# Three early up weights are split later at the norm of the output projection, in a two-layer hybrid decoder trunk

## The chip, the cores and the metric

The kernel runs on one core of one Trainium2 chip. The metric is the device time of one execution in microseconds (us). Five engines work side by side, each through its own queue in order: TensorE (PE: matrix products and transposes; its weight loads are listed as PEld), VectorE (DVE), ScalarE (ACT), GpSimd (POOL) and SyncE (SP), whose queue issues the loads from the chip's main memory here. An instruction that has to wait holds up everything behind it on its engine.

## The reference

The reference computes two layers on 512 tokens of width 1024, in float32. In each layer the residual stream goes through one input projection into three mixers (latent attention, causal pooling, a matrix-memory recurrence), whose outputs meet in one output projection. Then come a layer norm and a gated MLP, and a second norm:

```
mix = concat([a, p, m]) @ w_out[l]
h = layer_norm(ALPHA * h + mix, ln1_g[l], ln1_b[l])
a, g = split(h @ w_up[l], 2)            # 1024 -> 2 * 2816
g = causal_dwconv(g, w_fconv[l], b_fconv[l])
h = layer_norm(ALPHA * h + (silu(g) * a) @ w_down[l], ln2_g[l], ln2_b[l])
```

The change concerns the place between the second and the third of these lines: the norm behind the output projection, and the first products of the up projection.

## The kernel before

**Numbers in two parts.** A float32 product is made of three products: each operand is split into a high part (a cast on ScalarE to a shorter format) and a low part (VectorE subtracts the high part from the original), and high x high, high x low and low x high are added up. Activations are split by `split` (lines 187 to 189) into `a_hi` and `a_lo`, weights by `fetch` (lines 149 to 170).

**Weights.** All weights stand in one list in the order of their use. `getw` (line 174) hands out the next one and calls `fetch` for all up to `ahead` beyond it. `fetch` makes three instructions on three engines: a 512 KB load on SyncE's queue into a buffer `raw` (two buffers), the cast to `hi` on ScalarE (line 168), the subtraction to `lo` on VectorE (line 169). There are four `hi` and four `lo` buffers. A load waits for the `raw` buffer, which the subtraction of the weight two places earlier frees.

**The norm.** The 512 tokens are four tiles of 128, counted from 0. The second half of the output projection ends tile by tile, and for each tile `ln_tail` (line 208) follows: mean and variance on VectorE, the power -1/2 on GpSimd (line 200), the normalisation on VectorE (line 227), and then, twice (once for each half of the 1024 columns): four transposes on TensorE into one bank (line 238), four activations on ScalarE into a buffer `lnt` that apply gain and bias (line 243; two such buffers), and the split into `a_hi` (ScalarE, line 188) and `a_lo` (VectorE, line 189).

**The first up weights.** The up projection starts before all four tiles are normalised. `t_half` (line 313) takes the first four weights of the list, here called A, B, C and D. In its first half (`hf` 0) each is multiplied with tiles 0 and 1, in the second half (`hf` 1) with tiles 2 and 3. Each weight and half has two groups of four blocks (the first needs the first halves of the two tiles, the second their second halves), and each group three passes of four products: `hi` with `a_hi`, `lo` with `a_hi`, `hi` with `a_lo` (line 328). A is fetched earlier, during the output projection (`ahead=1` there). B, C and D are fetched in `t_half` itself, each just ahead of its first products, inside a `tc.issue_after` block.

**What sets the order.** The order of TensorE's instructions is that in which the program traces them; a small planner (`Order`) interleaves the generators by estimated costs. On the other engines the framework's scheduler sets the order when the program is built: of the instructions that are ready by its own clock it takes the one traced first, unless `high_priority` moves one forward (the norm's statistics and normalisation have that). `tc.issue_after(ins)` adds an edge of order, without a wait, to `ins` from each instruction that the block traces on the engine of `ins`, and leaves those on other engines alone. In `t_half` it names `last_rs[0]`, the last power that `rstd_of` gave to GpSimd.

Of the kernel before, what the change touches and what calls it, by code (L numbers as in the profile page):

```python
# [10 lines left out]
F32 = mybir.dt.float32  # L11
# [3 lines left out]
ALU = mybir.AluOpType  # L15
# [3 lines left out]
P = 128  # L19
# [82 lines left out]
def trunk(ctx: ExitStack, tc: tile.TileContext, I: dict, out: bass.AP, layers=DEPTH):  # L102
    nc = tc.nc
    V, A, G, T = nc.vector, nc.scalar, nc.gpsimd, nc.tensor
# [11 lines left out]
    a_hi = pers.tile([P, NT, KD, P], F32R, name="a_hi")  # L116
    a_lo = pers.tile([P, NT, KD, P], F32R, name="a_lo")
# [18 lines left out]
    def mmc(n):  # L136
        return n / 2400.0 + 0.003

    def bank(name):
        return psum.tile([P, S], F32, tag="ps", name=name)  # L140
# [33 lines left out]
    def getw(name, ahead=1):  # L174
        while len(wloaded) <= min(used[0] + ahead, len(wlist) - 1):
            fetch()
        hi, lo, nm = wloaded[used[0]]
        assert nm == name, (nm, name)
        used[0] += 1
        return hi, lo  # L180
# [4 lines left out]
        T.matmul(o, wlo, xhi, start=False, stop=stop)  # L185

    def split(hi, lo, src, eng=None):
        A.copy(hi, src)
        (eng or V).tensor_tensor(lo, src, hi.bitcast(F32), ALU.subtract)

    def load_gb(pool, gsrc, bsrc, name):
        gb = pool.tile([P, 2, D], F32, tag="gb", name="gb_" + name)
# [4 lines left out]
    def rstd_of(dst, src, eps):  # L197
        n = src.shape[1]
        V.tensor_scalar_add(dst, src, eps)
        return G.tensor_tensor(dst, dst, nhalf[:, :n], ALU.pow).ins  # L200
# [3 lines left out]

    dve_free = [0.0]
    last_rs = [None]

    def ln_tail(pool, h, i, st, gb, cols, name, transpose=True, dst=None, pre=1.3):
        mv = small.tile([P, 2], F32, tag="mv", bufs=4, name="mv_" + name)
        rs = small.tile([P, 1], F32, tag="rs", bufs=4, name="rs_" + name)  # L210
        with tc.high_priority(offset=2000):
            V.bn_aggr(mv, st)
            last_rs[0] = rstd_of(rs, mv[:, 1:2], LN_EPS)
        z = h[:, i, :]
        if not transpose:
            n = D // 2 if i == NT - 1 else D
            with tc.high_priority(offset=1000 if i == NT - 1 else 0):
                for a in range(0, D, n):
                    za = z[:, a : a + n]
                    V.scalar_tensor_tensor(za, za, mv[:, 0:1], gb[:, 0, a : a + n], ALU.subtract, ALU.mult)  # L220
                for a in range(0, D, n):
                    za = z[:, a : a + n]
                    V.scalar_tensor_tensor(za, za, rs[:, 0:1], gb[:, 1, a : a + n], ALU.mult, ALU.add)  # L223
                    (A if a else nc.sync).dma_start(dst[i * P : (i + 1) * P, a : a + n], za)
            return
        with tc.high_priority(offset=2000):
            V.tensor_scalar(z, z, mv[:, 0:1], rs[:, 0:1], ALU.subtract, ALU.mult)
        if dst is not None:
            nc.sync.dma_start(dst[i * P : (i + 1) * P, :], z)
        dve_free[0] = max(dve_free[0], sch.now) + pre + 1.5  # L230
        yield 0.0, dve_free[0] + 0.72 - sch.now, None
        for q in range(2):
            tp = bank("tp_" + name)
            t = pool.tile([P, S], F32, tag="lnt", bufs=2, name="lnt_" + name)
            for k in range(4):
                f = q * 4 + k
                ks = slice(k * P, (k + 1) * P)
                T.transpose(tp[:, ks], h[:, i, f * P : (f + 1) * P], ident)
            for k in range(4):
                f = q * 4 + k  # L240
                ks = slice(k * P, (k + 1) * P)
                w, b = cols[:, f : f + 1], cols[:, KD + f : KD + f + 1]
                A.activation(t[:, ks], tp[:, ks], AF.Identity, bias=b, scale=w)
            split(a_hi[:, i, q * 4 : q * 4 + 4, :], a_lo[:, i, q * 4 : q * 4 + 4, :],
                  t.rearrange("p (k t) -> p k t", t=P))
            yield 0.43, 0.0, None
        sch.set(f"hT_{name}_{i}", 3.82)

# [64 lines left out]
    def t_half(names, waits):  # L313
        ws, os_ = [], []
        for hf in range(2):
            t0, t1 = hf * 2, hf * 2 + 2
            for w in waits[hf]:
                yield 0.0, 0.0, w
            for n, nm in enumerate(names):
                if hf == 0:  # L320
                    with tc.issue_after(last_rs[0]):
                        ws.append(getw(nm, ahead=0))
                    os_.append(bank("t_" + nm))
                hi, lo = ws[n]
                for k0 in range(0, KD, 4):
                    for p_ in range(3):
                        for k in range(k0, k0 + 4):
                            T.matmul(os_[n][:, t0 * P : t1 * P], (lo if p_ == 1 else hi)[:, k * P : (k + 1) * P],  # L328
                                     (a_lo if p_ == 2 else a_hi)[:, t0:t1, k, :], start=k == p_ == 0,
                                     stop=k == KD - 1 and p_ == 2)  # L330
                    yield 12 * mmc(256), 0.0, None
                if hf == 1:
                    yield ("done", n, os_[n])
# [97 lines left out]
    for i in range(NT):  # L431
        for a in range(0, D, D // 2 if i == 0 else D):
            n = D // 2 if i == 0 else D
# [14 lines left out]
    def first_norm():  # L448
        for i in range(NT):
            st = new_stats("0")  # L450
            for j in range(2):
                ln_stats(h, i, j, st)
            yield from ln_tail(lp, h, i, st, None, cols0, "in0", dst=spill)
            if i == 0:
                warm(6)
# [28 lines left out]
    for l in range(layers):  # L484
# [31 lines left out]
        def rms(i, ps, n, gcol, hi, lo, nm):  # L516
            kd = None
            if nm == "cq":
                o = QL + 2 * MH
                kd = t2("kd")[:, : 2 * P]  # L520
                m1, m2 = kd[:, 0:ROPE], kd[:, ROPE : 2 * ROPE]
                V.tensor_mul(m1, ps[:, o : o + ROPE], cst_t[:, i, 0, :])
                V.tensor_mul(m2[:, 0:32], ps[:, o + 32 : o + 64], cst_t[:, i, 1, 0:32])
                V.tensor_mul(m2[:, 32:64], ps[:, o : o + 32], cst_t[:, i, 1, 32:64])
                V.tensor_tensor(kd[:, P : 2 * P].rearrange("p (a e) -> p a e", a=2),
                                m1.unsqueeze(1).to_broadcast([P, 2, ROPE]),
                                m2.unsqueeze(1).to_broadcast([P, 2, ROPE]), ALU.add)
            sq = t2("sq_" + nm)
            ss = small.tile([P, 1], F32, tag="ss", bufs=4, name="ss_" + nm)
            A.activation(sq[:, :n], ps[:, :n], AF.Square, scale=n ** -0.5, accum_out=ss)  # L530
            rs = small.tile([P, 1], F32, tag="rsq", bufs=4, name="rs_" + nm)
            rstd_of(rs, ss, RMS_EPS)
            V.scalar_tensor_tensor(sq[:, :n], ps[:, :n], rs[:, 0:1], gqkv[:, gcol : gcol + n], ALU.mult, ALU.mult)
            yield 0.0, 4.0 + 0.7 * i, None
            tp = bank("rt_" + nm)
            for k in range(n // P):
                T.transpose(tp[:, k * P : (k + 1) * P], sq[:, k * P : (k + 1) * P], ident)
            if kd is not None:
                T.transpose(tp[:, QL : QL + P], kd[:, P : 2 * P], ident)
                ts_ = slice(i * P, (i + 1) * P)  # L540
                split(kp_hi[:, ts_], kp_lo[:, ts_], tp[:, QL : QL + P])
            split(hi[:, :, i * P : (i + 1) * P], lo[:, :, i * P : (i + 1) * P],
                  tp[:, :n].rearrange("p (k t) -> p k t", t=P))
            yield n / P * 0.107, 0.0, None
            sch.set(f"{nm}{l}_{i}", 2.94)
# [498 lines left out]
        def ffn_main():  # L1044
            yield from until(o0)
            for y in out_gen(1):
# [4 lines left out]
                if last_grp and y[0] > 0 and pre_left:  # L1051
                    with tc.issue_after(lo_ins[f"o{l}_1_3"]):
                        hbox["pre"](pre_left.pop(0), 1)
            ffn_open()
            hbox["g1"] = load_gb(hp, I["ln1_g"][l], I["ln1_b"][l], "1")
            w1 = [[f"hT_a{l}_{i}" for i in range(2 * hf, 2 * hf + 2)] for hf in range(2)]
            yield from consume(t_half([f"up{l}_0_0", f"up{l}_0_1", f"up{l}_1_0", f"up{l}_1_1"], w1),
                               lambda n, o: up_consume(n // 2, n % 2, o))
            for n in range(4, 2 * NF):
# [116 lines left out]
```

## Time and profile before

| | us |
|---|---|
| three timed runs | 1143.2, 1141.77, 1143.14; median 1143.14 |
| the profiled execution | 1142.44 |
| its span, first to last instruction | 1140.7 |
| TensorE busy | 1118.5 (98%) |
| VectorE busy | 783.4 (69%) |
| ScalarE busy | 506.1 (44%) |
| GpSimd busy | 276.6 (24%) |

The stage of the change lies around 205 to 250 us in layer 0 and around 764 to 806 us in layer 1.

How to read it: the page's first part gives busy time, share of the span and number of instructions of each engine. A timeline lists instructions in order of time: start, duration, engine, line, operation, tile written and tiles read, and how many like ones were merged (x4); brackets hold the idle time of the engine ahead of the row, and what ended it. Matmuls overlap, so the pace is read from the starts, not from the durations. The chain of waits follows the work that ended last back through what released it. A table of windows gives, for stretches of time, the busy time of each engine and the granted clock of TensorE (1.00 is 2.4 GHz, 0.50 is 1.2 GHz). `t_up` are the banks of the up products, `hi_up`, `lo_up` and `raw_up` the up weights, `tp_a` the transposes of this norm.

### The profile page before, as it was taken

To read this page: it belongs to the slowest core of one execution; us is meant where nothing else is said; L and a number is where in the kernel's file an instruction comes from. 1 tells how busy PE (TensorE), PEld (TensorE's weight loads), DVE (VectorE), ACT (ScalarE), POOL (GpSimd) and SP (SyncE) were. 2 spreads that over 40 slices of the span, in tenths; PEclk is the share of its full clock that TensorE was granted. 3 is DMA by queue.
4 is the path that set the end of the run, shared out by engine and by line. 5 is a ranking of instruction groups with operands and counts; after the bars stand their busy time and mean duration, and the time that the engine had idled before them with its cause. 6 is when DMAs were issued, how large, how long until landed. Compare 5 with 4: busy or idle time off the path is not lost. (4 is left out here: it accounts for less than half of the span.)

```text
span 1140.7 us, 14294 instructions
## 1 busy us (share of the span) xinstructions
PE 1118.5 (98%) x5399; PEld 930.2 (82%) x5399; DVE 783.4 (69%) x1151; ACT 506.1 (44%) x870; POOL 276.6 (24%) x218
## 2 busy tenths in 40 slices
PE   8999999999999999999999999999999999999996
PEld 5878778798888888888887888888888888888885
DVE  6776886856696667844568669685777865696447
ACT  6664552553443444333266645517434334443320
POOL 1316500128320222011003362000663012220111
PEclk9999999999999999999999999999999999999999
DMA  8332215323415231433243213062432343215221
GB/s 302 107 107 63 88 38 203 126 78 93 140 60 191 90 109 58 129 125 97 92 155 130 66 34 110 24 243 67 120 122 91 118 154 98 93 56 166 93 74 74
DMA packets 36084, 124.96 MB, mean 110 GB/s; under 512 B 4521, under 2 KB 5033, under 8 KB 36017
## 3 DMA queue, kind: packets, MB, share of 16 engines
q1 hardware_dynamic: 35872, 123.80, 33.0%
q8 instruction: 42, 0.69, 0.3%
q10 hardware_dynamic: 144, 0.26, 0.1%
q14 instruction: 26, 0.21, 0.1%
HBM read 117.74 MB, written 6.31 MB: 109 GB/s over the span
## 5 line engine op out<-in xcount | busy, mean ns | idle before, releaser
L183 PE MATMUL t_up<-a_hi,hi_up 128*128 128x512 f32 x640 | 249.0, 389 | 0.0
L184 PE MATMUL t_up<-a_lo,hi_up 128*128 128x512 f32 x640 | 249.0, 389 | 0.0
L185 PE MATMUL t_up<-a_hi,lo_up 128*128 128x512 f32 x640 | 249.0, 389 | 0.0
L169 DVE TENSOR_TENSOR lo_up<-raw_up,hi_up 128x1024 fp32r<-128x1024 f32 x88 | 129.2, 1469 | 103.5 <-ACT hi_up L168 102.4
L168 ACT CAST hi_up<-raw_up 128x1024 fp32r<-128x1024 f32 x88 | 92.4, 1050 | 120.5 <-PE t_up L184 70.4
L184 PEld LDWEIGHTS t_up<-a_lo,hi_up 128*128 128x128 f32 x640 | 120.1, 188 | 25.0
L183 PEld LDWEIGHTS t_up<-a_hi,hi_up 128*128 128x128 f32 x640 | 120.1, 188 | 24.8
L185 PEld LDWEIGHTS t_up<-a_hi,lo_up 128*128 128x128 f32 x640 | 120.1, 188 | 24.8
L995 POOL TENSOR_TENSOR s_lo<-y,s_hi 128x256 fp32r<-128x256 f32 (+1 forms) x32 | 48.5, 1516 | 282.3 <-ACT s_hi L994 261.9
L972 ACT ACTIVATE y<-y 128x512 f32<-128x512 f32 x44 | 27.8, 632 | 107.4 <-DVE y L971 107.4
L971 DVE SCALAR_TENSOR_TENSOR y<-t_up,pp,y 128x511 f32<-128x511 f32 x88 | 65.5, 744 | 11.5 <-ACT y L969 10.2
L976 DVE TENSOR_TENSOR y<-y,t_up 128x512 f32<-128x512 f32 x44 | 30.2, 687 | 52.9 <-PE t_up L185 37.4
L980 POOL TENSOR_TENSOR f_lo<-y,f_hi 128x512 fp32r<-128x512 f32 x12 | 21.1, 1755 | 176.3 <-ACT f_hi L979 176.3
L169 DVE TENSOR_TENSOR lo_s<-sum,hi_s 128x1024 fp32r<-128x1024 f32 x32 | 43.3, 1354 | 14.6 <-ACT hi_s L168 14.6
L293 PE MATMUL o<-hi_o,a_hi 128*128 128x512 f32 x128 | 50.9, 398 | 0.0
L295 PE MATMUL o<-hi_o,a_lo 128*128 128x512 f32 x128 | 49.9, 390 | 0.0
L294 PE MATMUL o<-lo_o,a_hi 128*128 128x512 f32 x128 | 49.9, 390 | 0.0
L1033 PE MATMUL dx<-hi_s,s_hi 128*128 128x512 f32 x128 | 49.8, 389 | 0.0
L1034 PE MATMUL dx<-lo_s,s_hi 128*128 128x512 f32 x128 | 49.8, 389 | 0.0
L1035 PE MATMUL dx<-hi_s,s_lo 128*128 128x512 f32 x128 | 49.8, 389 | 0.0
L168 ACT CAST hi_s<-sum 128x1024 fp32r<-128x1024 f32 x32 | 33.6, 1052 | 30.3 <-PE dy L1035 13.4
L168 ACT CAST hi_s<-raw_s 128x1024 fp32r<-128x1024 f32 x24 | 25.3, 1055 | 39.9 <-PE dx L1035 21.5
(311 smaller groups left out, 2545.6 us busy)
## 6 DMA issues: line engine op xcount, KB each, us to landing
raw_up<-in_w_up_dram SPq DMA_DIRECT2D x88, 512.0 KB, 3.5
raw_s<-in_w_ds_dram SPq DMA_DIRECT2D x32, 512.0 KB, 3.5
raw_o<-in_w_out_dram SPq DMA_DIRECT2D x16, 512.0 KB, 3.5
raw_it<-in_w_it_dram SPq DMA_DIRECT2D x12, 512.0 KB, 3.6
raw_d<-in_w_dn_dram SPq DMA_DIRECT2D x12, 512.0 KB, 3.4
spill<-h SPq DMA_DIRECT2D x8, 512.0 KB, 4.0
raw_ib<-in_w_ib_dram SPq DMA_DIRECT2D x8, 512.0 KB, 3.5
h<-spill SPq DMA_DIRECT2D x8, 512.0 KB, 7.8
```

Of the source, the lines that this page charges most:

```text
L168: A.copy(h_, r_)
L169: lo_ins[name] = eng.tensor_tensor(l_, r_, h_.bitcast(F32), ALU.subtract).ins
L183: T.matmul(o, whi, xhi, start=start, stop=False)
L184: T.matmul(o, whi, xlo, start=False, stop=False)
L185: T.matmul(o, wlo, xhi, start=False, stop=stop)
L293: T.matmul(o, xhi, whi, start=at == 0, stop=False)
L294: T.matmul(o, xhi, wlo, start=False, stop=False)
L295: T.matmul(o, xlo, whi, start=False, stop=at == nk - 1)
L971: V.scalar_tensor_tensor(y[:, t:], o[:, : S - t], w(2 - t), y[:, t:], ALU.mult, ALU.add)
L1033: T.matmul(o, xhi, hi[:, w], start=new and pp == 0, stop=False, skip_group_check=True)
L1034: T.matmul(o, xhi, lo[:, w], start=False, stop=False, skip_group_check=True)
L1035: T.matmul(o, xlo, hi[:, w], start=False, stop=end, skip_group_check=True)
```

## The change

`split` returns its two instructions, and `ln_tail` keeps those of the last half of each tile in `tile_split`. In `t_half` the block around the fetch of the first weight (A, which is there already) keeps the edge to `last_rs[0]`. For the second to fourth weight (B, C, D) the edges go to the two instructions of tile 1's last split: their casts on ScalarE are queued behind that tile's last cast, and their subtractions on VectorE behind its last low part. The loads on SyncE's queue get no edge.

```diff
     def split(hi, lo, src, eng=None):
-        A.copy(hi, src)
-        (eng or V).tensor_tensor(lo, src, hi.bitcast(F32), ALU.subtract)
+        a = A.copy(hi, src).ins
+        return a, (eng or V).tensor_tensor(lo, src, hi.bitcast(F32), ALU.subtract).ins
...
     last_rs = [None]
+    tile_split = {}
...
-            split(a_hi[:, i, q * 4 : q * 4 + 4, :], a_lo[:, i, q * 4 : q * 4 + 4, :],
-                  t.rearrange("p (k t) -> p k t", t=P))
+            tile_split[i] = split(a_hi[:, i, q * 4 : q * 4 + 4, :], a_lo[:, i, q * 4 : q * 4 + 4, :],
+                                  t.rearrange("p (k t) -> p k t", t=P))
...
             for n, nm in enumerate(names):
                 if hf == 0:
-                    with tc.issue_after(last_rs[0]):
+                    with ExitStack() as hs:
+                        for ins in tile_split[1] if n else (last_rs[0],):
+                            hs.enter_context(tc.issue_after(ins))
                         ws.append(getw(nm, ahead=0))
```

## Rows read from the trace of the kernel before

**Rows 1.** The page, part 1: busy us, share of the span, instructions.

```profile
PE 1118.5 (98%) x5399; PEld 930.2 (82%) x5399; DVE 783.4 (69%) x1151; ACT 506.1 (44%) x870; POOL 276.6 (24%) x218
```

**Rows 2.** The chain of waits, layer 1's norm: start, us, what.

```profile
782.31 0.61 DVE a_lo L189
782.96 3.60 PE t_up L328 x28
```

**Rows 3.** Timeline of TensorE, layer 0: passes 1, 4, 6, 10, transposes, passes 14, 48.

```profile
219.07 0.72 PE L328 MATMUL t_up<-a_hi,hi_up 128*128 128x256 f32 x4
...
221.55 0.74 PE L328 MATMUL t_up<-a_hi,hi_up 128*128 128x256 f32 x4 [0.49 <-ACT a_hi L188]
...
224.35 1.22 PE L328 MATMUL t_up<-a_lo,hi_up 128*128 128x256 f32 x4 [1.59 <-DVE a_lo L189]
...
227.80 0.64 PE L328 MATMUL t_up<-a_hi,hi_up 128*128 128x256 f32 x4
...
229.22 1.03 PE L238 MATMUL tp_a<-ident,h 128*128 128x128 f32 x8
...
230.57 0.64 PE L328 MATMUL t_up<-a_hi,lo_up 128*128 128x256 f32 x4
...
246.88 0.64 PE L328 MATMUL t_up<-a_lo,hi_up 128*128 128x256 f32 x4
```

**Rows 4.** Timeline of TensorE, layer 1: passes 1 and 10.

```profile
777.68 0.72 PE L328 MATMUL t_up<-a_hi,hi_up 128*128 128x256 f32 x4
...
784.96 0.64 PE L328 MATMUL t_up<-a_hi,hi_up 128*128 128x256 f32 x4
```

**Rows 5.** Windows: PE, PEld, DVE, ACT, POOL busy; granted clock; DMA share; GB/s.

```profile
224.40:228.00 3.60, 3.60 (x18) 3.60 (x19) 2.33 (x3) 2.12 (x5) 0.00 (x0) 0.55 0.57 208
...
783.00:787.00 4.00, 4.00 (x34) 4.00 (x35) 2.52 (x3) 2.86 (x7) 0.00 (x0) 1.00 0.47 162
```

**Rows 6.** Timeline of ScalarE, layer 0: tiles 1 to 3, casts of B, C, D.

```profile
215.01 1.08 ACT L168 CAST hi_up<-raw_up 128x1024 fp32r<-128x1024 f32 x1
...
216.47 2.01 ACT L243 ACTIVATE lnt_a<-tp_a,pp 128x128 f32<-128x128 f32 x5
...
219.93 1.05 ACT L168 CAST hi_up<-raw_up 128x1024 fp32r<-128x1024 f32 x1
220.86 0.64 ACT L188 CAST a_hi<-lnt_a 128x512 fp32r<-128x512 f32 x1
221.38 1.52 ACT L243 ACTIVATE lnt_a<-tp_a,pp 128x128 f32<-128x128 f32 x4
222.76 1.07 ACT L168 CAST hi_up<-raw_up 128x1024 fp32r<-128x1024 f32 x1
...
229.86 1.85 ACT L243 ACTIVATE lnt_a<-tp_a,pp 128x128 f32<-128x128 f32 x5 [3.04 <-PE tp_a L238]
```

**Rows 7.** Timeline of VectorE, layer 0: B, C, tile 3's normalisation, tile 1's last a_lo.

```profile
217.84 1.22 DVE L169 TENSOR_TENSOR lo_up<-raw_up,hi_up 128x1024 fp32r<-128x1024 f32 x1
...
221.22 1.23 DVE L169 TENSOR_TENSOR lo_up<-raw_up,hi_up 128x1024 fp32r<-128x1024 f32 x1
222.89 0.81 DVE L227 TENSOR_SCALAR h<-h,mv_a,rs_a 128x1024 f32<-128x1024 f32 x1 [0.44 <-POOL rs_a L200]
223.61 0.68 DVE L189 TENSOR_TENSOR a_lo<-lnt_a,a_hi 128x512 fp32r<-128x512 f32 x1
```

**Rows 8.** Timeline of GpSimd, layer 0: the powers of tiles 2 and 3.

```profile
215.94 0.54 POOL L200 TENSOR_TENSOR rs_a<-rs_a,nhalf 128x1 f32<-128x1 f32 x1 [4.19 <-DVE rs_a L199]
221.38 1.47 POOL L200 TENSOR_TENSOR rs_a<-rs_a,nhalf 128x1 f32<-128x1 f32 x1 [4.90 <-DVE rs_a L199]
```

**Rows 9.** Timeline of SyncE's queue, layer 0: the load of D.

```profile
219.13 0.33 SPq L160 DMA_DIRECT2D raw_up<-in_w_up_dram  x1
```

**Rows 10.** The page, part 6: issues, KB each, median us to landing.

```profile
raw_up<-in_w_up_dram SPq DMA_DIRECT2D x88, 512.0 KB, 3.5
```

## Prediction

> **What bounds the kernel now.** I read four views, in this order. The first part of the page: TensorE is busy for 98% of the span [rows 1], so a microsecond is won only where TensorE stands still. The chain of waits in order of time tells where that is: from 782.96 us TensorE runs into itself almost to the end, and just ahead of it VectorE makes a low part a_lo [rows 2]. The timeline of TensorE shows the place: the first half of the up projection at the norm (line 328), once in each layer. The timelines of ScalarE, VectorE and GpSimd show why a_lo is late there.
>
> The unit is a pass: four matmuls of 256 columns. Undisturbed, 34 passes in layer 0 take 246.88 - 230.57 = 16.31 us, 0.48 each [rows 3]. A weight has six passes on the first two tiles: high, low and a_lo with the weight's first four blocks, then the same with the other four. Passes 1 to 6 belong to the first weight (A), which is split long before. Passes 7 to 12 belong to the second (B), then come tile 3's transposes (I count tiles from 0), then weights C and D. From pass 1 (219.07) to pass 10 (227.80) layer 0 takes 8.73 us where 9 x 0.48 = 4.32 would do: 4.41 us lost [rows 3]. Layer 1 takes 784.96 - 777.68 = 7.28: 2.96 lost [rows 4]. The loss lies ahead of pass 6: from pass 1 to it each layer takes 5.28 (224.35 - 219.07, and 782.96 - 777.68 [rows 2 to 4]) where 2.40 would do, 2.88 lost. Most of it is two waits, ahead of pass 4 for tile 1's second cast and ahead of pass 6 for its low part a_lo: the rows put 0.49 and 1.59 to them [rows 3]; the rest is a short wait for an earlier a_lo and the slower pass (0.56) after each stop.
>
> The 1.45 us that layer 0 loses beyond layer 1 is clock: behind the same wait the granted clock was 0.55 of full speed from 224.40 to 228.00, mostly the 1.2 GHz level, and 1.00 (2.4 GHz) in layer 1 [rows 5]. The Trainium skill ("TensorE: Matmul & The Clock Gate", "What's actually happening") says that the point at which the clock changes shifts from run to run, as the chip's watch is not tied to the program. The two layers agree with it; by that rule the 1.45 belongs to no version, and the sum below would be 1.45 less favourable.
>
> **The change, part by part.** The new edges set an order on an engine and add no instruction. The old edge behind last_rs named a GpSimd instruction, and a weight's fetch has nothing on GpSimd here (a load on SyncE's queue, a cast on ScalarE, a subtraction on VectorE): taking it away costs 0.
>
> *What goes.* In layer 0 ScalarE casts B at 215.01 and C at 219.93, both ahead of tile 1's second cast at 220.86; each takes 0.93 from its start to the next start [rows 6]. VectorE does B's low part at 217.84 and C's at 221.22; tile 3's normalisation follows (222.89), and only then tile 1's last a_lo (223.61 to 224.29) [rows 7]. With both casts gone from the front, tile 1's second cast starts 2 x 0.93 sooner, near 219.0, and ends near 219.65. Its a_lo can start as soon as that, or behind tile 3's statistics, which VectorE has to do in that time, near 220.9 (an estimate: in before the power that follows them started at 221.38 [rows 8], with 0.5 of B's low part ahead of them); so it ends between 220.4 and 221.6. TensorE wants the cast for pass 4 at 220.6 and the a_lo for pass 6 at 221.55. So the waits go: up to 2.88 us per layer, and layer 0's 1.45 with them if the clock then holds.
>
> *What comes.* B now stands behind that cast, and behind B stand its own low part, D's load, and pass 7. Tile 2's eight activations were traced before B and are ready by then. Where B's cast lands among them the trace of before does not show, so I bound it. Early end: directly behind tile 1's cast, 219.0 + 0.52 = 219.5. Late end: behind tile 2's eight activations and first cast, which take what tile 1's took, 219.93 - 216.47 = 3.46 [rows 6]: 223.0. Between them lies the gap after tile 2's first four activations (221.38 to 222.76 is 1.38): 220.9. I take the late end. In before ScalarE went from four activations straight to a fifth where the next lnt buffer was free (x5 at 216.47), and took a weight where it wasn't (x4 at 221.38, D at 222.76) [rows 6]; the buffer is freed by tile 1's a_lo, which now is done about when the four end.
>
> Then B's cast runs 223.0 to 224.05; its low part starts 1.29 after the cast's start (221.22 - 219.93) and takes 1.23 [rows 6, 7], so it ends at 225.5. Pass 7 is due at 219.07 + 0.56 + 5 x 0.48 = 222.05 and comes at 224.1, 2.05 late; pass 8 needs the low part and is 0.95 late more. With three restarts the loss is 3.2 us per layer. Layer 0: 3.2 - 4.4 = -1.2. Layer 1: 3.2 - 2.96 = +0.25. **Sum -0.95.**
>
> *What hides the rest.* C's cast follows tile 2's last one, about 224.4 to 225.5, low part by 226.9; TensorE wants it after tile 3's transposes, near 228.8: covered by 2 us. D: its load waits for the raw buffer that B's low part frees (in before 217.84 + 1.22 = 219.06, issue 219.13 [rows 7, 9]) and takes 3.5 [rows 10]. So D is in at 229.0 instead of 222.6; it is wanted at 231.7. That cover is thin: the second rival. Behind D's load on SyncE's queue stand only later up loads, whose split waits for a buffer until the second half of the stage.
>
> **The rivals.**
>
> *B goes early (faster).* If B's cast takes the gap at 220.9, its low part ends at 223.4; pass 7 is in time, pass 8 is 0.95 late, and the loss is 1.1 per layer: (1.1 - 4.4) + (1.1 - 2.96) = -5.15. At 219.5 nothing is late: (0.1 - 4.4) + (0.1 - 2.96) = -7.2. For it: in before ScalarE did place D behind four activations of tile 2 [rows 6]. Against it: the buffer named above, and D's wait as below would eat it (then -0.15, which I count to the forecast). It also hangs on the order on VectorE. If tile 3's normalisation stays ahead of tile 1's a_lo as in before [rows 7], it must wait for GpSimd's power, which took 1.47 us for tile 3 and 0.54 for tile 2 [rows 8]. Say it starts 0.5 sooner than in before, near 220.9, as B's low part no longer stands ahead of tile 3's statistics. At 0.54 the normalisation starts at 221.5, a_lo 0.72 later [rows 7], and ends at 222.9: pass 6 is 1.4 late, pass 8 0.2, the loss is 1.85 per layer, and the -5.15 shrinks to -3.7. At 1.47 pass 6 is 2.3 late, the loss 2.7, and -2 is left.
>
> The Trainium skill ("SBUF — State Buffer", "Who interferes with whom") says that a VectorE instruction with two SBUF inputs and a GpSimd one that reads SBUF shut each other out, the second waiting for the first. The trace agrees: the 1.47 began 0.16 after C's low part and ended 0.4 after it [rows 7, 8]. By the rule the short time holds once C's low part is out of that place.
>
> *D comes late (slower).* The transposes of tile 3 follow pass 12, at 227.95 in the forecast; ScalarE starts on tile 3 0.64 later (229.22 to 229.86 in before [rows 3, 6]), at 228.6, and D's weights land at 229.0. If ScalarE's order has tile 3's work first, D's cast waits 3.46: 232.05 to 233.1, low part to 234.6. TensorE wants D at 231.7: 1.45 late, and its low part 0.9 more, 2.5 with restarts, in both layers: -0.95 + 5.0 = +4.05, before any fall of the clock (1.45 each). It decides wherever D lands behind the start of tile 3's activations; by my times the two are 0.4 us apart. For it: tile 3's work was traced before D. Against it: ScalarE idles from 225.5 to 228.6, so an order that expects the load a little sooner puts D in front, and then nothing is lost.
>
> *Nothing moves.* If the named split were one done much earlier, the order would stay. Tile 1's entry is overwritten just before, in the same layer, so I give it little: 0, 1142.4.
>
> **How the numbers follow.** The profiled execution took 1142.44 us, 1.74 more than its span; the median of the three runs is 1143.14, so 0.70 is added to compare with it. Forecast: 1143.14 - 0.95 = 1142.2, its own range 1140.3 (a little of the early case) to 1145.1 (the clock falls in both layers): chance 0.45. B early: 1138.0, between 1135.9 and 1141: 0.33. D late: 1147.2: 0.19. Nothing moves: 1143.1: 0.03. A difference of 0.2%, 2.3 us, is what a measurement of this kernel can tell. Faster by more than that: nearly all of 0.33 and a tenth of the forecast, 0.37. Slower: most of 0.19 and a little of the forecast, 0.21. Between: 0.42. The range from 1136.8 to 1147.0 takes in most of the two rivals.
>
> **What would show it.** Right: in both layers line 328 waits no more for a_lo of tile 1; its longest wait, about 2 us, is for the cast of B, followed by one of 1 us for B's low part; ScalarE's cast of B stands behind tile 2's eight activations. B's cast behind tile 2's first four says the fast rival. A wait of line 328 after tile 3's transposes, for D, says the slow one. The prediction is wrong in its ground if a wait for tile 1's a_lo over 1 us stays.

## The result: slower by half a per cent, and the profile after

Six timed runs of the changed kernel gave 1145.78 to 1150.19 us, median 1147.37; six of the kernel before gave 1141.77 to 1143.2, median 1142.93. The ratio is 1.0051, with a 95% interval of 1.004 to 1.0063. The forecast was 1142.2 with a range up to 1147.0: the kernel became slower, where no change that can be measured was the likeliest case. What came is the rival "D comes late", whose price was 1147.2.

The profiled execution took 1150.17 us (span 1148.4), at the upper end of the six. TensorE's busy time rose by 3.8 us, and its share stays 98% (answers to [rows 1]):

```profile
PE 1122.3 (98%) x5399; PEld 933.2 (81%) x5399; DVE 782.5 (68%) x1151; ACT 505.6 (44%) x870; POOL 276.8 (24%) x218
```

TensorE's waits (line waited for: us in total, times, longest). Line 328 is line 331 now. No wait for a_lo or a cast of tile 1 is left there. In their place stand eight waits for weights:

```profile
PE t_up L331 <- ACT hi_up L168: 6.1, 4, 1.9
PE t_up L331 <- DVE lo_up L169: 2.1, 4, 0.5
```

TensorE's timeline in layer 0 shows where (answers to [rows 3]). The rows are passes 1, 6, 7, 8, 18, 19, 20, 25 and 48:

```profile
219.02 0.72 PE L331 MATMUL t_up<-a_hi,hi_up 128*128 128x256 f32 x4
...
221.50 0.64 PE L331 MATMUL t_up<-a_lo,hi_up 128*128 128x256 f32 x4
224.05 0.74 PE L331 MATMUL t_up<-a_hi,hi_up 128*128 128x256 f32 x4 [1.91 <-ACT hi_up L168]
225.31 0.74 PE L331 MATMUL t_up<-a_hi,lo_up 128*128 128x256 f32 x4 [0.52 <-DVE lo_up L169]
...
231.06 0.64 PE L331 MATMUL t_up<-a_lo,hi_up 128*128 128x256 f32 x4
232.84 0.73 PE L331 MATMUL t_up<-a_hi,hi_up 128*128 128x256 f32 x4 [1.15 <-ACT hi_up L168]
234.10 1.15 PE L331 MATMUL t_up<-a_hi,lo_up 128*128 128x256 f32 x4 [0.52 <-DVE lo_up L169]
...
238.10 0.64 PE L331 MATMUL t_up<-a_hi,hi_up 128*128 128x256 f32 x4
...
249.13 0.64 PE L331 MATMUL t_up<-a_lo,hi_up 128*128 128x256 f32 x4
```

The reader is to see that passes 1 to 6 now run at the full pace (2.48 us from the first to the sixth start, where it was 5.28), and that pass 7 (B's high part), 8 (B's low part), 19 and 20 (the same of D) each start late: by 2.07, 0.78, 1.30 and 0.78 us against the pace of 0.48. That is 4.93 us in this layer, where 2.88 were lost before. Layer 1 has the same four waits.

ScalarE's timeline in layer 0 shows why (answers to [rows 6]): tile 1's second cast, tile 2's work, the casts of B and C, tile 3's work, the cast of D:

```profile
219.12 0.62 ACT L188 CAST a_hi<-lnt_a 128x512 fp32r<-128x512 f32 x1
219.64 1.85 ACT L244 ACTIVATE lnt_a<-tp_a,pp 128x128 f32<-128x128 f32 x5
...
221.88 1.18 ACT L244 ACTIVATE lnt_a<-tp_a,pp 128x128 f32<-128x128 f32 x3
222.92 1.08 ACT L168 CAST hi_up<-raw_up 128x1024 fp32r<-128x1024 f32 x1
...
224.38 1.09 ACT L168 CAST hi_up<-raw_up 128x1024 fp32r<-128x1024 f32 x1
228.43 1.85 ACT L244 ACTIVATE lnt_a<-tp_a,pp 128x128 f32<-128x128 f32 x5 [2.97 <-PE tp_a L239]
230.16 0.64 ACT L188 CAST a_hi<-lnt_a 128x512 fp32r<-128x512 f32 x1
230.67 1.19 ACT L244 ACTIVATE lnt_a<-tp_a,pp 128x128 f32<-128x128 f32 x3
231.71 1.08 ACT L168 CAST hi_up<-raw_up 128x1024 fp32r<-128x1024 f32 x1
```

B's cast starts at 222.92. VectorE (answers to [rows 7]) makes tile 1's last a_lo 3.6 us sooner than before, but B's low part now ends at 225.26, and at 225.28 the queue of SyncE issues D's load (answers to [rows 9]):

```profile
220.00 0.67 DVE L189 TENSOR_TENSOR a_lo<-lnt_a,a_hi 128x512 fp32r<-128x512 f32 x1
...
224.03 1.23 DVE L169 TENSOR_TENSOR lo_up<-raw_up,hi_up 128x1024 fp32r<-128x1024 f32 x1 [0.98 <-ACT hi_up L168]
...
232.82 1.23 DVE L169 TENSOR_TENSOR lo_up<-raw_up,hi_up 128x1024 fp32r<-128x1024 f32 x1 [1.30 <-ACT hi_up L168]
```

```profile
225.28 0.33 SPq L160 DMA_DIRECT2D raw_up<-in_w_up_dram  x1
```

With 3.5 us to landing (an estimate: the median in [rows 10]) D is in at 228.8. ScalarE began tile 3 at 228.43, about 0.35 us sooner, and its fixed order takes all eight activations and a cast before D.

It is this order, settled when the program was built, that makes D wait, and not the 0.35 us: in layer 1 D's load is issued at 786.43 and lands 3.5 us later, at 789.9, while ScalarE stands still. Tile 3's transposes come late there (the clock had fallen, as shown below), and still D's cast comes only behind tile 3's work (ScalarE's timeline, layer 1; the bracket is its idle time):

```profile
791.09 1.86 ACT L244 ACTIVATE lnt_a<-tp_a,pp 128x128 f32<-128x128 f32 x5 [4.49 <-PE tp_a L239]
...
794.38 1.08 ACT L168 CAST hi_up<-raw_up 128x1024 fp32r<-128x1024 f32 x1
```

So D had been in for 1.2 us when ScalarE took the first activation of tile 3.

The chain of waits of layer 1 (start, us, what; answers to [rows 2]) tells the same in one piece. B's cast and low part hold TensorE, TensorE holds tile 3's transposes, these hold tile 3's work on ScalarE, and that work holds D's cast and low part:

```profile
784.21 0.94 ACT hi_up L168
...
785.17 1.24 DVE lo_up L169
...
786.46 4.08 PE t_up L331 x20
790.53 0.54 PE tp_a L239 x4
...
791.45 1.50 ACT lnt_a L244 x4
792.96 0.51 ACT a_hi L188
793.46 1.06 ACT lnt_a L244 x3
794.52 0.94 ACT hi_up L168
...
795.49 1.24 DVE lo_up L169
...
796.77 3.29 PE t_up L331 x16
```

The rest of the profiled execution's loss comes with a lower granted clock. The windows behind D's wait in layer 0, and behind B's and D's in layer 1 (columns as in [rows 5]), show a granted clock well below 1.00:

```profile
234.10:238.10 4.00, 4.00 (x21) 4.00 (x21) 0.55 (x1) 0.00 (x0) 0.00 (x0) 0.57 0.40 131
787.03:791.25 4.22, 4.22 (x27) 4.22 (x25) 1.11 (x1) 0.16 (x1) 0.00 (x0) 0.60 0.72 230
796.77:801.24 4.47, 4.47 (x25) 4.47 (x25) 0.55 (x1) 0.00 (x0) 0.00 (x0) 0.62 0.43 117
```

The five passes from 234.10 to 238.10 took 4.00 us where 2.40 would do: 1.6, of which 0.1 is the slower pass behind every wait. From pass 1 to pass 48 the stage took 27.81 and 26.38 us in the two layers before, and takes 30.11 and 31.63 after: 7.55 us more, of the 7.7 by which the spans differ. All the rest of the kernel together comes to 0.15. The best stage of the experiments below, without waits and at full clock, takes 23.50. Measured against it, the waits with the slower pass behind them cost 10.2 us in the two layers after and 5.8 before, 4.5 more (rounded), and the falls of the clock 4.5 and 1.4, 3.1 more. The medians of the timed runs differ by 4.4, which is about the waits alone.

### The profile page after: what moved, and what is told of

Read it like the earlier page. It is cut to its first block, busy times and chain, and to the rows that moved or that the text cites. A ratio compares the mean times of both kernels' runs of the same rounds, so it can differ in the third digit from the quotient of the medians.

```text
span 1148.4 us, 14290 instructions
## 1 busy us (share of the span) xinstructions
PE 1122.3 (98%) x5399; PEld 933.2 (81%) x5399; DVE 782.5 (68%) x1151; ACT 505.6 (44%) x870; POOL 276.8 (24%) x218
## 4 chain that ended last, share of the span: by engine, by line
PE 84%; DVE 9%; ACT 3%; POOL 2%; issue 1%; DMA 1%; SPq 0%; DVEq 0%; POOLq 0%; ACTq 0%
PE t_up L183 13%; PE t_up L185 13%; PE t_up L184 13%; PE t_up L331 3%; PE dx L1037 3%; PE dx L1036 3%; PE dx L1038 3%; PE ia L283 2%; PE o L294 2%; PE o L296 2%; PE o L295 2%; PE d L296 2%; PE d L295 2%; PE d L294 2%; PE dy L1036 1%
```

## The experiments

The theory: one cause, B's place on ScalarE. Its late cast makes its low part late, this makes D's load late by way of the raw buffer, and D's cast then falls behind tile 3's activations. All versions below are edits of the changed kernel. "Stage" is the time from pass 1 to pass 48 in layer 0 and layer 1. The kernel before has 27.81 and 26.38, the changed one 30.11 and 31.63.

The ratios are to runs of the kernel before on the same chip as each version (medians 1142.93, 1142.16 for the next four, 1141.92 for the last two).

| version | median us (runs) | ratio to before, 95% interval | stage |
|---|---|---|---|
| changed kernel | 1147.37 (6) | 1.0051 [1.004, 1.0063] | 30.11, 31.63 |
| D in a buffer of its own | 1142.99 (12) | 1.0008 [0.9998, 1.0017] | 27.93, 26.44 |
| edges on C and D only | 1137.08 (6) | 0.9955 [0.9941, 0.9968] | 23.80, 23.80 |
| edges, and priority for B, C, D | 1135.35 (6) | 0.9942 [0.9929, 0.9955] | 23.50, 23.50 |
| edges on VectorE only | 1144.32 (12) | 1.002 [1.001, 1.0029] | 28.79, 28.83 |
| edges, and priority for D | 1143.8 (10) | 1.0014 [1.0004, 1.0023] | 27.52, 27.99 |
| edges, and priority for B | 1135.67 (4) | 0.9939 [0.9922, 0.9955] | 23.65, 23.65 |

**D in a buffer of its own.**

```diff
-                raw = stream.tile([P, CH], F32, tag="raw", bufs=2, name="raw_" + name)[:, :n]
+                own = name in [f"up{l_}_1_1" for l_ in range(layers)]
+                pool, tag = (pools["f"], "raw2") if own else (stream, "raw")
+                raw = pool.tile([P, CH], F32, tag=tag, bufs=2, name="raw_" + name)[:, :n]
```

> The changed kernel, but weight D (the fourth) is loaded into a buffer of its own, so that its load no longer waits for B's low part; all edges stay. Theory (B's late cast makes B's low part late, this makes D's load late, and D's cast then falls behind tile 3's activations): D's cast stands right behind C's and the waits ahead of pass 19 and 20 (1.30 and 0.78 us per layer, with restarts 2.25) go, those for B stay (2.07 and 0.78); 4.5 us less than the changed kernel and a fall of the clock less: about 1142. Rival 1 (D is late because of its own edge, not its load): no change, 1147. Rival 2 (the clock, not the waits, makes the loss): between, 1145 to 1147, with the falls still there behind B.

It came to 1142.99, 1 us above the figure expected. ScalarE casts C and D in one run, ahead of tile 3 (first fence, its timeline), and TensorE waits at this line (333 there) for B's two parts alone (second fence, its waits):

```profile
225.07 2.03 ACT L170 CAST hi_up<-raw_up 128x1024 fp32r<-128x1024 f32 x2
```

```profile
PE t_up L333 <- ACT hi_up L170: 3.8, 2, 1.9
...
PE t_up L333 <- DVE lo_up L171: 1.0, 2, 0.5
```

D's edge is there as in the changed kernel, so the edge does not make D late; the buffer does. The layers of this run differ by 1.5, again by one fall of the clock. The interval of the ratio takes in 1: with D covered, the exchange of tile 1's waits for B's is about even, as the forecast had it.

**Edges on C and D only.**

```diff
-                        for ins in tile_split[1] if n else (last_rs[0],):
+                        for ins in tile_split[1] if n > 1 else (last_rs[0],):
```

> The changed kernel without the edges on B: only C and D go behind tile 1's split. Theory: B's cast and low part go back to their early place, so nothing of B or D is late; C's cast and low part no longer stand ahead of tile 1's second cast and a_lo, so these come near 220.6 and 221.5 and TensorE's waits ahead of pass 4 and 6 go but for a few tenths. Loss about 0.4 us per layer instead of 4.4 and 2.96 before: 1136 to 1137.5, faster than both. Rival (any weight behind tile 1 is late for TensorE): a wait for C ahead of pass 13 of over 1 us per layer, 1140 or more.

1137.08, in the expected range, and no wait of 0.2 us or more at line 331. A stage of 23.80 is 0.3 above the best seen here. That is pass 3, which still starts 0.2 late, as B's low part keeps a place ahead of an earlier a_lo.

**Edges and priority for B, C and D.**

```diff
                             hs.enter_context(tc.issue_after(ins))
+                        if n:
+                            hs.enter_context(tc.high_priority(offset=1000))
```

> The changed kernel, all edges kept, but the fetches of B, C and D have priority over tile 2's and 3's activations, so that B stands directly behind tile 1's last cast (near 219.6) and not behind tile 2's eight activations. Theory (what costs is only the place behind tile 2's work): no wait at line 331 over 0.3 us, loss 0.1 to 0.4 us per layer, 1135.5 to 1137. Rival (work behind the edge is late wherever it stands): B's low part still makes pass 8 wait by over 0.5 us, 1140 or more.

1135.35, a little under the expected range. ScalarE takes B and C together right behind tile 1's second cast, and tile 2 after them:

```profile
220.55 0.62 ACT L188 CAST a_hi<-lnt_a 128x512 fp32r<-128x512 f32 x1
221.07 1.99 ACT L168 CAST hi_up<-raw_up 128x1024 fp32r<-128x1024 f32 x2
222.97 1.85 ACT L244 ACTIVATE lnt_a<-tp_a,pp 128x128 f32<-128x128 f32 x5
```

All the edges of the change are in, and no wait of 0.2 us or more is left in this stage: the edges themselves cost nothing. What cost was the place that the scheduler then found for B.

**Edges on VectorE only.**

```diff
-                        for ins in tile_split[1] if n else (last_rs[0],):
+                        for ins in tile_split[1][1:] if n else (last_rs[0],):
```

> The changed kernel with the edges on VectorE alone: the low parts of B, C and D stand behind tile 1's last a_lo, the casts are free as before. Theory: the casts of B and C return to the front, TensorE waits about 0.95 us for tile 1's cast and 0.4 for its a_lo; B's low part ends near 224.1, so D's load is still late and D's cast falls behind tile 3's activations: waits of 1.35 and 0.7 us for D. Loss about 3.9 us per layer: 1143 to 1145, with D's wait and no wait for B over 0.3 us. Rival (D is late because of its edge on ScalarE): D is cast early, loss 1.7 per layer, 1138 to 1139.5.

1144.32, in the expected range. B and C are cast early again (B at 214.73, C at 219.66), yet D is cast behind tile 3, at 230.19, and TensorE waits for it as in the changed kernel. The rows are D's cast on ScalarE and passes 19 and 20 on TensorE:

```profile
230.19 1.08 ACT L168 CAST hi_up<-raw_up 128x1024 fp32r<-128x1024 f32 x1
```

```profile
231.31 0.74 PE L331 MATMUL t_up<-a_hi,hi_up 128*128 128x256 f32 x4 [1.14 <-ACT hi_up L168]
232.58 1.22 PE L331 MATMUL t_up<-a_hi,lo_up 128*128 128x256 f32 x4 [0.53 <-DVE lo_up L169]
```

D has no edge on ScalarE here, and is late. So the edge on its cast is not needed for that; B's late low part, which holds D's load back, is enough.

**Edges and priority for D; edges and priority for B.** Both are the edit of the third version, with `if n == 3:` and with `if n == 1:`.

> The changed kernel, all edges and the late load of D kept, but D's fetch has priority, so that its cast may stand in front of tile 3's activations but for the first. Theory (D's price comes from the order of ScalarE: its load lands only about 0.4 us behind the start of tile 3's work, and the 3.46 us of that work are then taken first): D's cast starts near 228.9 instead of 231.7 on the changed kernel's clock, D's waits go as with the buffer of its own, B's stay: 1142 to 1144. Rival (the late load itself is the price): D still waits over 1 us, 1146 to 1147.5.

> The changed kernel, all edges kept, but B's fetch alone has priority, so that its cast stands directly behind tile 1's last one; C and D are placed as they come. Theory (one cause: B's place; D is late only because B's low part is): no wait for B, D's load goes out near 222.2 and its cast stands ahead of tile 3's activations, no wait for D either: 1135 to 1136.7, as with priority for all three. Rival (D's place is a cause of its own, as its edge or its order puts it behind tile 3): B's waits go but D's 2.25 us per layer stay, 1139 to 1141.

With priority for D the time is 1143.8, in the expected range. D's load is as late as ever, but its cast stands behind one activation of tile 3 instead of eight, and no wait for D is left: TensorE waits in this stage for B's two parts alone, 3.9 and 0.7 us in all. The rows are ScalarE's timeline:

```profile
229.83 0.46 ACT L244 ACTIVATE lnt_a<-tp_a,pp 128x128 f32<-128x128 f32 x1 [4.00 <-PE tp_a L239]
230.19 1.04 ACT L168 CAST hi_up<-raw_up 128x1024 fp32r<-128x1024 f32 x1
```

With priority for B alone it is 1135.67, in the expected range too: no wait for B, and none for D either, though D has no priority. On ScalarE B's cast stands right behind tile 1's second one (218.86), and D's ahead of tile 3's work:

```profile
218.86 0.62 ACT L188 CAST a_hi<-lnt_a 128x512 fp32r<-128x512 f32 x1
219.39 1.04 ACT L168 CAST hi_up<-raw_up 128x1024 fp32r<-128x1024 f32 x1
...
225.26 1.05 ACT L168 CAST hi_up<-raw_up 128x1024 fp32r<-128x1024 f32 x1
226.22 1.85 ACT L244 ACTIVATE lnt_a<-tp_a,pp 128x128 f32<-128x128 f32 x5
```

That makes B's place the one cause and D's lateness its consequence. Three versions beat both kernels: the two that put B right behind tile 1's cast (priority for B, C and D, and for B alone) are 0.6% faster than the kernel before, the one with the edges on C and D only 0.45%.

## Why the prediction was wrong

The steps that held, in the order of the text:

- That the old edge did nothing, and that tile 1's split would come sooner: its cast starts at 219.12 (near 219.0 was written), and both its waits are gone.
- Where B lands: behind tile 2's eight activations, the late end of the bounds, at 222.92 (223.0 was written). Its low part ends at 225.26 (225.5). Passes 7 and 8 are 2.07 and 0.78 us late (2.05 and 0.95; the sum for pass 7's due time gives 222.03, where 222.05 stands). With two restarts of 0.08 that is 3.0 per layer, where 3.2 stood in the sum. The forecast stood for a kernel with D covered, which the version with D's own buffer is. Its stage is 27.93 and 26.44, 0.2 us more in all than before, each with one fall of the clock; the forecast's -0.95 had assumed that this fall goes. Its time came out 0.9 above before, with an interval from -0.2 to +1.9.
- D's load: issued at 225.28, in at 228.8 (229.0 was written); tile 3's activations from 228.43 (228.6).

**The step that failed** is the last sentence of "D comes late": "ScalarE idles from 225.5 to 228.6, so an order that expects the load a little sooner puts D in front, and then nothing is lost". The forecast counted D as covered on that ground and left this rival 0.19. The order that was built has tile 3's work first, and D's cast waited for eight activations and a cast. In layer 0 the two events were about 0.35 us apart (0.4 was written). But the rival went by the times on the chip ("It decides wherever D lands behind the start of tile 3's activations"), and layer 1 shows that these don't decide: there D was in 1.2 us before ScalarE began tile 3, and its cast still came behind that work. The order was settled when the program was built; when the scheduler expected the load is not on record. With priority for D the cast stands behind one activation of tile 3; by the rule of the order (of the ready instructions the one with priority goes first) that fits a scheduler that had D ready just after tile 3's work, but it is not shown.

The price was nearly right: D cost about 2.2 us per layer (1.30, 0.78 and the slower pass behind them) where 2.5 was written. That the total agrees, 1147.2 against 1147.37, is partly luck. The waits of B and D were put about 1 us too high in the two layers together, and against that stands the gain of 1.45 for layer 0's clock, which the profiled run did not show. What was wrong was the chance, and the range's upper end: 1147.0 lies 0.2 below this rival's own bare price, so the range left out most of it, and with it the falls of the clock that the text names. A cover of 0.4 us between two events that are both estimated to some tenths is no cover. With no row that told how the scheduler would place D, the two cases should have shared their 0.64 about evenly, which makes slower about as likely as faster.

The other rivals: "B goes early" did not happen by itself, but its price did hold when the place was forced: -7.2 was written for B directly behind tile 1's cast, and the two versions with that order have ratios of 0.9942 and 0.9939, 6.6 and 7.0 us of 1142. "Nothing moves" did not happen.

The clock: the prediction said that a fall costs 1.45 and belongs to no version. The size holds (1.5 for the one worked out above). The second half is not borne out: in the profiled runs, one for each version, the three versions without waits have no fall in this stage in either layer, the kernel before and the one with D's own buffer have one, the versions with edges on VectorE only and with priority for D two, the changed kernel three. The falls came only where there were waits, though not behind every wait: in the changed kernel B's in layer 0 had none.

## What to carry to other kernels

An edge that moves one instruction back also moves what its buffer lets in: follow the buffer to the next load, and the next load to its own place in each queue, before calling the move covered. The order of an engine is settled when the program is built, and the engine keeps to it even where an urgent load is in first (by 1.2 us in layer 1 here). When eight small instructions become ready at about the moment at which that load is due, the urgent one can wait for none of them or for all; give it the priority outright instead of leaving it to the order that falls out. To free the front of a queue, move only what is not needed soon (C and D here), or move it and say where it is to go (B right behind the split).

## What the runs showed of the hardware

The granted clock fell to between 0.57 and 0.62 on average for 4.0 to 4.5 us behind three of the four pairs of waits (1.15 to 1.92 us and 0.5 us close by), at about 1.5 us lost for the one in layer 0.

The timed runs of one kernel differ in their mean granted clock, and their times go with it. For the changed kernel it was 0.993 in the two longest runs (1150.17 and 1150.19) and 0.995 or 0.996 in the other four (1145.78 to 1147.57). For the kernel before, in the 23 runs to which the first four edited versions are compared, it was 0.998 in ten (1140.49 to 1142.22) and 0.994 or 0.995 in the four longest (1143.67 to 1145.09). Where in a run the clock fell only the profiled runs show. The spread does not simply follow the number of waits in this stage: 4.4 us for six runs of the changed kernel, which has eight, 4.6 for those 23 of the kernel before, which has four, 1.6 for six runs of the version with priority for B, C and D, which has none.

GpSimd's power of 128 x 1 elements took 0.54 us for tile 3 in the changed kernel, where it took 1.47 before [rows 8], and 0.99 for tile 2, where it took 0.54. Both moved as VectorE's two-input subtractions did (the timelines of GpSimd and, below it, of VectorE):

```profile
215.89 0.99 POOL L200 TENSOR_TENSOR rs_a<-rs_a,nhalf 128x1 f32<-128x1 f32 x1 [3.94 <-DVE rs_a L199]
221.06 0.54 POOL L200 TENSOR_TENSOR rs_a<-rs_a,nhalf 128x1 f32<-128x1 f32 x1 [4.17 <-DVE rs_a L199]
```

```profile
215.80 0.69 DVE L189 TENSOR_TENSOR a_lo<-lnt_a,a_hi 128x512 fp32r<-128x512 f32 x1
```

An a_lo started 0.09 before tile 2's power and ended 0.39 before the power's end; nothing stood beside tile 3's. That is what the Trainium skill ("SBUF — State Buffer", "Who interferes with whom") says of two such instructions, one of VectorE with two SBUF inputs and one of GpSimd that reads SBUF, and the trace agrees with it. Here it cost nothing, as TensorE did not wait for these tiles.
